# A hybrid decoder layer on one core: dense products placed between the steps of its RWKV-7 branch, and zeros, a scaling and stores moved

## The chip, the core and the metric

The kernel runs on one core of a Trainium2 chip. A core has five engines that each work through a queue of their own in order: PE (matrix products; the trace shows its weight loads apart, as PEld), DVE (elementwise work, reductions), ACT (activation functions and copies), POOL (elementwise work, zeroing) and SP (used here for issuing DMA transfers). [...] The metric is the device time of one execution in microseconds, lower is better.

## The reference, cut to what matters

One layer of a decoder for 512 prompt tokens and 64 tokens of eight running sequences (576 columns in all). The normalised input is multiplied with one large matrix `w_in`; of its columns, some feed an RWKV-7 branch, some a differential attention, some two sigmoid gates. Both branches are gated, added, multiplied with `w_out`, and a squared-ReLU MLP follows. The change lies in the RWKV branch and beside it:

```python
def step(S, inp):
    r_t, w_t, k_t, v_t, a_t, b_t = inp
    sa = jnp.einsum('bhij,bhj->bhi', S, a_t)
    S = S * w_t[:, :, None, :] + sa[..., None] * b_t[:, :, None, :] + v_t[..., None] * k_t[:, :, None, :]
    return S, jnp.einsum('bhij,bhj->bhi', S, r_t)
...
kk = kk / jnp.maximum(jnp.linalg.norm(kk, axis=-1, keepdims=True), 1e-12)
S, y = rwkv7_scan(S0, hs(r), hs(decay), hs(k), hs(v), -kk, kk * hs(a))
mean = jnp.mean(y, axis=-1, keepdims=True)
var = jnp.mean(jnp.square(y - mean), axis=-1, keepdims=True)
y = (y - mean) * lax.rsqrt(var + GN_EPS) * ln_x_w + ln_x_b
o = (y + bonus).reshape(B, T, W_A) * g
...
m = gate_a * (o_a @ lp['w_br_a']) + gate_b * (o_b @ lp['w_br_b'])
```

There are eight heads of 64, a state of 64 x 64 for each head and sequence.

## The kernel before, in words

Weights are streamed from memory in pieces of 512 columns. For each output block of 128 channels the generator `stream` (line 150 and on) loads the weights on SP's queue (`raw`), splits them on ACT and DVE into a rounded high part and a low part (`hi`, `lo`), and then *yields before each matmul*: 8 input blocks x 2 halves of 288 columns x 3 products (high x high, high x low, low x high) are 48 matmuls. These are the **dense products**; in the trace they write `ps_z` (columns of `w_in` for RWKV, function `shifted`), `ps_g` (gates, `gate`), `ps_brb` (output of the attention branch, `branch_b`), and later `ps_bra`, `ps_wo` and so on. Generators wait in a list, `waiting`, in one fixed order; each asks for the next only when the one before is spent, and the sums of one block go to one bank of accumulators, two banks in turn, so dense products never pass each other.

`take(n)` takes the next n dense products from the list where it stands in the program. Nothing binds them to that place: the planner that orders each engine's queue ahead of time walks the program in a simulation and gives an engine the next instruction that is ready there, so such products are drawn forward into any hole that the simulation sees. `fill(n)` does the same inside `tc.issue_after(ring["mm"].ins)`: its matmuls stand in PE's queue behind the last matmul that the program wrote before. `issue_after` orders a block's instructions that run on the same engine as the named one.

The eight heads are worked in four **pairs** (hp 0 to 3, the first to the fourth pair; two heads fill the 128 rows). `rwkv(hp)` is a generator with these stages, each ended by a `yield`:

- stage 0: squares of k, their sums per head on PE (`pn`), the power -1/2 on POOL (`nr`), spread to columns on POOL (`nb`), transposed on PE (`pk`); decay and gate terms (`pw`, `pa`, `u`, `aa`, a running sum `cum`); normalised keys `kk`, bonus sums (`rkp`, `pbn`, `bv`), and the products of keys within chunks of 64 tokens (`pA`, masked on DVE into `ABR` and `ST`). `ST` is zeroed in halves on POOL (line 818).
- stage 1: transposes of v (`pV`, into `SVU`) and of the keys (`pK`, into `KBt`), the starting states `s0` loaded and multiplied (`pI`), an identity block and zeros put into `SVU` on POOL (lines 871 and 872).
- stage 2: inversion of a triangular matrix by blocks of 32: `DT`, `Y`, `X`, then in four rounds `pW` and `pZ`, each followed by nine bound dense products (`blocks`); the result is `TT`, partly zeroed on POOL (lines 923 and 924).
- stage 3: states of the running sequences (`vm`, `pF`); stage 4: mean and variance of y (`var`, with a power on POOL, line 243); stage 5: scaling of y by var, transposes back (`pTy`), gating (`pg`), output.

`chain(pr)` walks the nine chunks of two pairs together, one after the other (`pch`, `pY`), each step needing the one before. At the end of the file's middle part a list written by hand sets the program order: `run(2, 3)` takes the next stage of hp 2 and of hp 3, and `take(n)` stands between. Before the change `fill(8)` stands after `pn` and after `pa` of stage 0 (for the third pair, `take(8)` instead), in stage 1 between `pV` and `pK` for the third and the fourth pair, and ahead of `pI` for the fourth (for the others `take(8)`).

`gate` stores each finished gate block to memory on SP's queue (line 452); they are read back much later.

Of the kernel before, what the change touches and what calls it, by code (L numbers as in the profile page):

```python
# [15 lines left out]
P = 128  # L16
# [20 lines left out]
C_ID, C_OB, C_M, C_MS, C_LM, C_I32, C_HS, C_SEL, C_MB, C_CM, C_END = (  # L37
    0, 128, 256, 384, 512, 672, 704, 706, 738, 746, 748)
# [3 lines left out]
def tile_hybrid_step(ctx, tc, xT, xsT, ktab, vtab, s0T, ptab, w_in, vecs, w2a2, g2, lamv,  # L42
                     w_bra, w_brb, w_out, w_up, w_down, cst, bias_p, bias_s,
                     yT, kTo, vTo, Sp, Ss, sh):
    nc = tc.nc
    PE, VE, AE, GE = nc.tensor, nc.vector, nc.scalar, nc.gpsimd
# [8 lines left out]
    ring = {"job": 0}  # L55

    def act(out, in_, func=AF.Copy, **kw):
        ring["act"] = AE.activation(out=out, in_=in_, func=func, **kw)  # L58

    def tt(out, a, b, op, eng=None):  # L60
        ins = (eng or VE).tensor_tensor(out=out, in0=a, in1=b, op=op)  # L61
        if eng is None:
            ring["tt"] = ins

    def stt(out, a, s, b, op0, op1):
        VE.scalar_tensor_tensor(out=out, in0=a, scalar=s, in1=b, op0=op0, op1=op1)

    def ts(out, a, s1, op0, s2=None, op1=ALU.bypass, eng=None):
        (eng or VE).tensor_scalar(out=out, in0=a, scalar1=s1, scalar2=s2, op0=op0, op1=op1)

    def mm(out, lhsT, rhs, start=True, stop=True):
        ring["mm"] = PE.matmul(out=out, lhsT=lhsT, rhs=rhs, start=start, stop=stop)  # L72
        return ring["mm"]
# [17 lines left out]
    MUL, ADD, SUB, MAX = ALU.mult, ALU.add, ALU.subtract, ALU.max  # L91
# [9 lines left out]
    def bank(name):  # L101
        return psw.tile([P, 512], F32, tag="w", name=name)

    def tbank(name):
        return psc.tile([P, 512], F32, tag="t", name=name)
# [6 lines left out]
    c = const.tile([P, C_END], F32, name="cst_sb")  # L112
# [21 lines left out]
    def v(i, n=1):  # L134
        return vec[:, i:i + n]
# [80 lines left out]
    def take(n):  # L216

        while waiting and n:
            if next(waiting[0], None) is None:
                waiting.pop(0)  # L220
            else:
                n -= 1

    def fill(n):

        with tc.issue_after(ring["mm"].ins):
            take(n)
# [37 lines left out]
    gt_d = tc.dram_tile([2 * KT, P, NT], F32, name="gt_d")  # L265
# [178 lines left out]
    def gate(g):  # L444

        gg = gs.tile([P, NT], F32, tag="gg", name=f"gg{g}")

        def ev(ps, t0, n):
            tt(gg[:, t0:t0 + n], ps, R1[:, t0:t0 + n], MUL)
            act(gg[:, t0:t0 + n], gg[:, t0:t0 + n], AF.Tanh, scale=0.5)  # L450
        yield from stream(w_in[26 + g], KT, xh, xl, HALF, ev, f"g{g}")
        nc.sync.dma_start(out=gt_d[g], in_=gg)

    def ob_halves():

# [209 lines left out]
    for h in range(HB):  # L665
        if h:
            qkv(h)
        for cc in range(2):
            GE.tensor_copy(
                out=qbd[64 * cc:64 * cc + 64, :, h, 8 * cc:8 * cc + 8],  # L670
                in_=qT[64 * cc:64 * cc + 64, h, NPR:].rearrange("p (b q) -> p b q", b=NB))
# [47 lines left out]
    def ch(a):  # L719
        return a.rearrange("p (c t) -> p c t", t=64)  # L720

    def m3(ap_, n):
        q, w = ap_.shape
        return ap_.rearrange("p (o w) -> p o w", o=1).broadcast_to([q, n, w])
# [17 lines left out]
    def rwkv(hp):  # L742
# [5 lines left out]
        def tmp(tag, bufs=1):  # L748
            return rt.tile([P, NT], F32, tag="T", name=f"{tag}_{hp}", bufs=6)


        sq = tmp("sq")
        act(sq, k, AF.Square, scale=v(V_KK + hp))
        pn = bank(f"pn{hp}")
        for t, o in enumerate(toks):
            mm(pn[:, 2 * t:2 * t + 2], sq[:, o:o + P], c[:, C_HS:C_HS + 2])
        (fill if hp != 2 else take)(8)
        nr = stat.tile([P, 10], F32, tag="nr", name=f"nr{hp}")
        ts(nr, pn[:, 0:10], 1e-24, MAX)
        GE.tensor_tensor(out=nr, in0=nr, in1=mhalf[:, :10], op=ALU.pow)  # L760

        nb = rt.tile([P, 5, P], F32, tag="G", name=f"nb{hp}", bufs=3)
        GE.tensor_copy(out=nb.rearrange("p t (a d) -> p (t a) d", a=2),
                       in_=nr.rearrange("p (a o) -> p a o", o=1).broadcast_to([P, 10, 64]))
        u = tmp("u")
        aa = tmp("aa")
        for t0, n in HALF:
# [3 lines left out]
            pa = bank(f"pa{hp}{t0}")  # L771
            mm(pa[:, :n], al[:, hs], Pt[12][:, t0:t0 + n])
            act(aa[:, t0:t0 + n], pa[:, :n], AF.Tanh, scale=0.5, bias=hw0[:, 4 + hp:5 + hp])
        (fill if hp != 2 else take)(8)
        ts(u, u, 1.0, ADD)
        cum = tmp("cum")
        VE.tensor_tensor_scan(out=cum, data0=reset, data1=u, initial=0.0, op0=MUL, op1=ADD)
# [36 lines left out]
        for par, rows in halves:  # L814
            stt(KB[rows, :, par], ch(aa)[rows], 0.5, ch(pinv)[rows], MUL, MUL)
            tt(KB[rows, :, 1 - par], ch(k2)[rows], ch(pinv)[rows], MUL)
            st = rb_.tile([P, NCH, 2, 64], F32, tag=f"ST{par}", name=f"ST{par}_{hp}")
            GE.memset(st[64 - 64 * par:128 - 64 * par], 0.0)
            stt(st[rows, :, 0], ch(kk)[rows], -1.0, ch(pm)[rows], MUL, MUL)
            tt(st[rows, :, 1], ch(r)[rows], ch(pe)[rows], MUL)  # L820
            ST.append(st)
# [4 lines left out]
        for par in range(2):  # L826
            rows = slice(64 * par, 64 * par + 64)
# [14 lines left out]
        SVU = own["SVU"][:, :, e]  # L842
        for cs, pV in two_chunks(f"pV{hp}", vv):
            for a, c0, c1 in cs:
                src = pV[64 * a:64 * a + 64].rearrange("p (c w) -> p c w", w=P)[:, :(c1 - c0 + 1) // 2]
                act(SVU[64:128, c0:c1:2, 0], src[:, :, 0:64])
                act(SVU[0:64, c0:c1:2, 1], src[:, :, 64:128])
        if hp >= 2:
            fill(8)
        KBt = rb_.tile([P, NCH, 2, 64], F32, tag="KBt", name=f"KBt{hp}")  # L850
        for c0, cn in ((0, 4), (4, 4), (8, 1)):
# [5 lines left out]

        s0 = rt.tile([P, NB, 64], F32, tag="s0", name=f"s0_{hp}")
        nc.sync.dma_start(out=s0, in_=s0T[hp])
        (fill if hp == 3 else take)(8)  # L860
        pI = bank(f"pI{hp}")
        for b in range(NB):
            for par, rows in halves:
# [2 lines left out]
        for par in range(2):  # L866
            rows = slice(64 * par, 64 * par + 64)
            for a in range(2):
                act(ST[par][rows, 8, a].rearrange("p (b t) -> p b t", b=NB),
                    pI[rows, 0:P].rearrange("p (b a t) -> p b a t", b=NB, a=2)[:, :, a])  # L870
            GE.tensor_copy(out=SVU[rows, 8, par], in_=c[rows, C_ID + 64 * par:C_ID + 64 * par + 64])
            GE.memset(SVU[rows, 0, par], 0.0)

        yield

# [10 lines left out]
        def blocks(ps, lhs, rhs, n):  # L886
            for ci in range(n):
                for g in range(4):
                    gs = slice(32 * g, 32 * g + 32)
                    last = mm(ps[gs, ci * 32:ci * 32 + 32], lhs[gs, ci], rhs[gs, ci])  # L890
            with tc.issue_after(last.ins):
                take(9)
            return ps[:, :n * 32].rearrange("p (c s) -> p c s", c=n)
# [3 lines left out]
        for l in range(1, 5):  # L897

            n = NCH if l < 3 else 8
            DM = rt.tile([P, NCH, 32], F32, tag="DM", name=f"DM{hp}_{l}")  # L900
            tt(DM[:, :n], DT[:, :n], m3(c[:, C_LM + 32 * l:C_LM + 32 * l + 32], n), MUL)
            W = rt.tile([P, NCH, 32], F32, tag="W", name=f"W{hp}_{l}")
            act(W[:, :n], blocks(tbank(f"pW{hp}{l}"), DM, X, n))
            tt(X[:, :n], X[:, :n], blocks(tbank(f"pZ{hp}{l}"), Y, W, n), ADD)
            VE.transpose(out=Y[:, :n], in_=X[:, :n])
        TT = rb_.tile([P, NCH, 64], F32, tag="TT", name=f"TT{hp}")
        pW = tbank(f"pWc{hp}")
# [11 lines left out]
        for b0, b1 in quads:  # L919
            act(TT[b0, :8, 32:64], pC[b0, :256].rearrange("p (c s) -> p c s", c=8))  # L920
            act(TT[b0, :, 0:32], Y[b0])
            act(TT[b1, :, 32:64], Y[b1])
            GE.memset(TT[b0, 8:, 32:64], 0.0)
            GE.memset(TT[b1, :, 0:32], 0.0)

        own[e] = ST, KBt, TT, ABR, pc
        yield
# [16 lines left out]
        y = own["y"][:, e]  # L944
# [4 lines left out]
        b9 = lambda a: a.rearrange("p (c o) -> p c o", o=1).broadcast_to([P, NCH, 64])  # L949
# [3 lines left out]
        var = stat.tile([P, NCH], F32, tag="var", name=f"var{hp}")  # L953
# [1 line left out]
        rpow(var, var, 1.0 / 64, 64e-5)  # L955

        yield
        tt(y, y, b9(var), MUL)
        oa = rt.tile([P, NT], F32, tag="G", bufs=3, name=f"oa{hp}")
        if hp >= 2:  # L960
            half_rows(hp)
# [79 lines left out]


    gens = [rwkv(hp) for hp in range(4)]

    def run(*stages):
        for hp in stages:
            while Pt[8 + hp] is None:
                take(2)
            next(gens[hp], None)

    waiting += zs(2) + zs(3) + [gate(g) for g in range(KT, 2 * KT)]
    ga = [gate(g) for g in range(KT)]
    waiting += ga[:5]
    run(0, 0)
    take(221)
    run(0, 1, 1)
    take(106)
    run(1)
    chain(0)
    run(2, 0, 1)  # L1060
    take(190)
    run(2, 3)
    take(85)
    run(2, 0, 1, 3)
    take(38)
    run(3)
# [21 lines left out]
    for d in range(KT):  # L1088
        g = []
        for i in range(2):  # L1090
            gg = rt.tile([P, NT], F32, tag="T", name=f"g{i}_{d}", bufs=6)
# [32 lines left out]
    for i, d in enumerate((0, 4, 1, 5, 2, 6, 3, 7)):  # L1124
# [31 lines left out]
        for j, (t0, n) in enumerate(HALF):  # L1156
            o = acc[:, t0:t0 + n]
# [142 lines left out]
    rows = []  # L1300
    for d, n in enumerate((None, "t1", "b11", "t2", "b21", "t3", "b22", "t4")):
        if n:
            t = fp.tile([P, 2, 4, 288], F32R, tag=f"h_{n}", name=f"w3_{d}", bufs=1)
            t = t.rearrange("p i k t -> p (i k t)")
# [179 lines left out]
```

## Time and profile before

| what | value |
|---|---|
| median of the timed runs | 1004.63 us (1004.32 to 1005.11, 3 runs) |
| the profiled execution's own time | 1006.88 us |
| its span, first to last instruction | 1005.1 us |
| PE busy | 975.1 us |
| DVE, ACT, POOL busy | 688.9, 497.0, 87.5 us |
| mean granted clock of PE | 0.993 |

A row of a group or of the timeline gives start and duration in microseconds, engine, line, operation, the tile written and the tiles read, their shapes, and how many instructions were merged (x4). In brackets stands the idle time of the engine just before, and what ended it. A row of a stretch gives, from one time to another, the busy time and the number of instructions of each engine, the granted clock of PE (1.00 is full), the share of the DMA engines and GB/s. Two matmul records of the trace belong to one product of 32-bit operands, one to a dense product. Matmuls overlap, so the start of one to the start of the next is what one costs.

### The profile page before, as it was taken

What the parts mean: (1) busy time and instruction counts of PE and PEld (TensorE: products, weight loads), DVE (VectorE), ACT (ScalarE), POOL (GpSimd) and SP (SyncE); (2) the same over time, 40 slices, a digit from 0 to 9 for tenths busy, and PEclk for the clock granted to TensorE, in tenths of its full rate; (3) what the DMA queues carried; (4) which work ended last, traced back from release to release, by engine and by line L of the source; (5) the groups of instructions that cost most, each with busy time, mean ns of one, the idle gap of its engine ahead of it and who ended that gap; (6) DMA issues with size and microseconds to landing.
All of it is one profiled execution on the core that took longest, in us unless ns stands there. A gap on an engine that the chain in (4) does not pass through costs nothing.

```text
span 1005.1 us, 24415 instructions
## 1 busy us (share of the span) xinstructions
PE 975.1 (97%) x10012; PEld 919.4 (91%) x10012; DVE 688.9 (69%) x1459; ACT 497.0 (49%) x1094; POOL 87.5 (9%) x171
## 2 busy tenths in 40 slices
PE   9999999899999998999989999999999999999996
PEld 9999998898887887988779999999999999999996
DVE  6698566864946679444579898966666666666644
ACT  6576455354435355453334666644444444444732
POOL 2511001301010340000210000000000000000001
PEclk9999999999989999999999999999999999999999
DMA  7422673211111234323357642222222222221402
GB/s 266 136 70 83 205 223 114 61 64 45 43 59 45 69 106 152 104 81 113 103 182 225 206 140 86 83 95 85 88 92 85 85 84 85 84 87 41 135 3 95
DMA packets 50833, 105.75 MB, mean 105 GB/s; under 512 B 6066, under 2 KB 8114, under 8 KB 50594
## 3 DMA queue, kind: packets, MB, share of 16 engines
q1 hardware_dynamic: 47442, 96.95, 30.4%
q0 software_dynamic: 1648, 5.35, 1.5%
q8 instruction: 79, 1.29, 0.5%
q10 hardware_dynamic: 1632, 1.89, 0.5%
q14 instruction: 32, 0.26, 0.1%
HBM read 89.38 MB, written 14.78 MB: 104 GB/s over the span
## 4 chain that ended last, share of the span: by engine, by line
PE 83%; DVE 6%; ACT 4%; issue 3%; DMA 2%; POOL 1%; SPq 0%; DVEq 0%; ACTq 0%; POOLq 0%
PE ps_dn L72 20%; PE ps_g L72 8%; PE ps_z L72 8%; PE ua L1220 5%; PE ux L1220 5%; PE ps_wo L72 4%; PE ps_k L72 3%; PE uc L1220 3%; PE ub L1220 3%; PE ud L1220 2%; PE ps_bra L72 2%; PE ps_q L72 2%; PE pch L72 2%; PE ps_brb L72 2%; PE ps_v L72 2%
## 5 line engine op out<-in xcount | busy, mean ns | idle before, releaser
L72 PE MATMUL ps_dn<-q,hi_dn 128*128 128x288 f32 x768 | 154.7, 296 | 0.0
L72 PEld LDWEIGHTS ps_dn<-q,hi_dn 128*128 128x128 f32 x768 | 122.7, 188 | 1.4
L72 PE MATMUL ps_dn<-q,lo_dn 128*128 128x288 f32 x384 | 113.2, 295 | 0.0
L72 PE MATMUL ps_g<-xl,hi_g 128*128 128x288 f32 x256 | 79.7, 311 | 0.0
L72 PE MATMUL ps_g<-xh,hi_g 128*128 128x288 f32 x256 | 79.0, 309 | 0.0
L72 PE MATMUL ps_g<-xh,lo_g 128*128 128x288 f32 x256 | 79.0, 309 | 0.0
L72 PEld LDWEIGHTS ps_dn<-q,lo_dn 128*128 128x128 f32 x384 | 72.0, 188 | 0.0
L72 PE MATMUL ps_z<-xh,lo_z 128*128 128x288 f32 (+1 forms) x224 | 68.9, 308 | 0.0
L72 PE MATMUL ps_z<-xh,hi_z 128*128 128x288 f32 (+1 forms) x224 | 67.6, 302 | 0.0
L72 PE MATMUL ps_z<-xl,hi_z 128*128 128x288 f32 (+1 forms) x224 | 66.8, 298 | 0.0
L61 DVE TENSOR_TENSOR ya<-ya,ps_dn 128x288 f32<-128x288 f32 x96 | 43.2, 451 | 29.4 <-PE ps_dn L72 29.4
L58 ACT ACTIVATE hi_dn<-raw_dn 128x512 fp32r<-128x512 f32 x48 | 30.1, 628 | 57.0 <-PE ps_dn L72 57.0
L1220 PE MATMUL ua<-h_b,hi 128*128 128x288 f32 x256 | 53.2, 298 | 0.0
L1220 PE MATMUL ux<-h_t,hi 128*128 128x288 f32 x256 | 52.3, 296 | 0.0
L58 ACT ACTIVATE c<-c 128x288 f32<-128x288 f32 x112 | 48.4, 439 | 7.4 <-DVE c L61 5.8
L72 PEld LDWEIGHTS ps_g<-xh,hi_g 128*128 128x128 f32 x256 | 48.7, 190 | 3.1 <-issue 1.8
L72 PEld LDWEIGHTS ps_g<-xl,hi_g 128*128 128x128 f32 x256 | 48.6, 190 | 1.9
L72 PEld LDWEIGHTS ps_g<-xh,lo_g 128*128 128x128 f32 x256 | 48.6, 190 | 1.6 <-DVE lo_g L61 0.2
L58 ACT ACTIVATE hi<-a 128x1024 fp32r<-128x1024 f32 (+1 forms) x32 | 27.1, 846 | 42.0 <-PE ps_dn L72 34.2
L72 PE MATMUL ps_dn<-q,w 128*128 128x320 f32 (+1 forms) x336 | 46.3, 297 | 0.0
L61 DVE TENSOR_TENSOR lo<-s,hi 128x1024 fp32r<-128x1024 f32 x32 | 39.2, 1224 | 10.1 <-ACT hi L58 10.0
L72 PEld LDWEIGHTS ps_dn<-q,w 128*128 128x128 f32 x336 | 45.3, 190 | 0.1
(395 smaller groups left out, 2802.2 us busy)
## 6 DMA issues: line engine op xcount, KB each, us to landing
a<-in_w_up_dram SPq DMA_DIRECT2D x32, 512.0 KB, 3.4
raw_dn<-in_w_down_dram SPq DMA_DIRECT2D x64, 256.0 KB, 2.8
raw_g<-in_w_in_dram SPq DMA_DIRECT2D x32, 256.0 KB, 3.1
raw_z<-in_w_in_dram SPq DMA_DIRECT2D x28, 256.0 KB, 3.1
gt_d<-gg SPq DMA_DIRECT2D x16, 288.0 KB, 2.4
g<-gt_d SPq DMA_DIRECT2D x16, 288.0 KB, 3.6
kp<-in_ktab_dram SPq DMA_DIRECT2D x16, 256.0 KB, 4.5
vp<-in_vtab_dram SPq DMA_DIRECT2D x16, 256.0 KB, 3.8
```

Source lines behind the costliest of these rows:

```text
L58: ring["act"] = AE.activation(out=out, in_=in_, func=func, **kw)
L61: ins = (eng or VE).tensor_tensor(out=out, in0=a, in1=b, op=op)
L72: ring["mm"] = PE.matmul(out=out, lhsT=lhsT, rhs=rhs, start=start, stop=stop)
L1220: ring["mm"] = PE.matmul(out=ps[:, :288], lhsT=l[:, k], rhs=hb[blk][:, h, k], start=start and i == 0, stop=i == 11, skip_group_check=skip)
```

## The change

1. Second pair (hp 1): its stage 1 no longer stands right after its stage 0 but behind the floating products, of which there are 82 instead of 106; eight bound products are put between `pV` and `pK`, and the eight ahead of `pI` become bound.
2. Third pair: the two groups of eight in stage 0 become bound.
3. Fourth pair: eight bound products are put ahead of `pn`; the floating products after its stage 0 are 77 instead of 85.
4. The zeros of the first pair in `ST`, `SVU` and `TT`, and for all pairs the identity copy into `SVU`, are queued on POOL behind the copy `nb` that was written last. The other pairs' zeros are as before.
5. The scaling of y in stage 5 stands in an `issue_after` that names a matmul: for the first two pairs the last one of the third round of the inversion written last (`ring["mid"]`), for the other two the last matmul written.
6. `gate` stores on ACT's queue instead of SP's.

```diff
         yield from stream(w_in[26 + g], KT, xh, xl, HALF, ev, f"g{g}")
-        nc.sync.dma_start(out=gt_d[g], in_=gg)
+
+        nc.scalar.dma_start(out=gt_d[g], in_=gg)
...
+        def clear(a):
+
+            if hp:
+                GE.memset(a, 0.0)
+            else:
+                with tc.issue_after(ring["nb"].ins):
+                    GE.memset(a, 0.0)
...
         pn = bank(f"pn{hp}")
+        if hp == 3:
+            fill(8)
         for t, o in enumerate(toks):
             mm(pn[:, 2 * t:2 * t + 2], sq[:, o:o + P], c[:, C_HS:C_HS + 2])
-        (fill if hp != 2 else take)(8)
+        fill(8)
...
-        GE.tensor_copy(out=nb.rearrange("p t (a d) -> p (t a) d", a=2),
-                       in_=nr.rearrange("p (a o) -> p a o", o=1).broadcast_to([P, 10, 64]))
+        ring["nb"] = GE.tensor_copy(out=nb.rearrange("p t (a d) -> p (t a) d", a=2),
+                                    in_=nr.rearrange("p (a o) -> p a o", o=1).broadcast_to([P, 10, 64]))
...
-        (fill if hp != 2 else take)(8)
+        fill(8)
         ts(u, u, 1.0, ADD)
...
-            GE.memset(st[64 - 64 * par:128 - 64 * par], 0.0)
+            clear(st[64 - 64 * par:128 - 64 * par])
...
-        if hp >= 2:
+        if hp >= 1:
             fill(8)
         KBt = rb_.tile([P, NCH, 2, 64], F32, tag="KBt", name=f"KBt{hp}")
...
-        (fill if hp == 3 else take)(8)
+        (fill if hp in (1, 3) else take)(8)
         pI = bank(f"pI{hp}")
...
-            GE.tensor_copy(out=SVU[rows, 8, par], in_=c[rows, C_ID + 64 * par:C_ID + 64 * par + 64])
-            GE.memset(SVU[rows, 0, par], 0.0)
+            with tc.issue_after(ring["nb"].ins):
+                GE.tensor_copy(out=SVU[rows, 8, par], in_=c[rows, C_ID + 64 * par:C_ID + 64 * par + 64])
+            clear(SVU[rows, 0, par])
...
             tt(X[:, :n], X[:, :n], blocks(tbank(f"pZ{hp}{l}"), Y, W, n), ADD)
+            if l == 3:
+                ring["mid"] = ring["mm"]
             VE.transpose(out=Y[:, :n], in_=X[:, :n])
...
-            GE.memset(TT[b0, 8:, 32:64], 0.0)
-            GE.memset(TT[b1, :, 0:32], 0.0)
+            clear(TT[b0, 8:, 32:64])
+            clear(TT[b1, :, 0:32])
...
         yield
-        tt(y, y, b9(var), MUL)
+
+        with tc.issue_after((ring["mid"] if hp < 2 else ring["mm"]).ins):
+            tt(y, y, b9(var), MUL)
...
     take(221)
-    run(0, 1, 1)
-    take(106)
-    run(1)
+    run(0, 1)
+    take(82)
+    run(1, 1)
     chain(0)
     run(2, 0, 1)
     take(190)
     run(2, 3)
-    take(85)
+    take(77)
     run(2, 0, 1, 3)
```

## The prediction

> **What bounds the kernel now.** I read the page's shares and its chain first, then the stretches of the RWKV part one by one, and inside a stretch the timeline.
>
> ```profile
> span 1005.1 us, 24415 instructions
> PE 975.1 (97%) x10012; PEld 919.4 (91%) x10012; DVE 688.9 (69%) x1459; ACT 497.0 (49%) x1094; POOL 87.5 (9%) x171
> ...
> PE 83%; DVE 6%; ACT 4%; issue 3%; DMA 2%; POOL 1%; SPq 0%; DVEq 0%; ACTq 0%; POOLq 0%
> ```
>
> PE is the bound: 975.1 of 1005.1 us busy, 83% of the chain that ended last. No matmul is added or removed, so the change can only win or lose PE's idle time (30 us in all), time in which PE works at a lower clock, and nothing else. The stretches (columns: busy time and count of PE, PEld, DVE, ACT, POOL, then the granted clock) tell where PE loses time among the parts that the diff touches:
>
> ```profile
> 178.20:182.30 4.10, 1.46 (x10) 1.17 (x8) 2.51 (x3) 2.19 (x4) 4.07 (x5) 1.00 0.00 0
> 262.00:271.70 9.70, 9.64 (x77) 9.15 (x75) 9.47 (x20) 2.56 (x5) 0.10 (x1) 1.00 0.19 57
> 271.70:276.70 5.00, 3.77 (x62) 3.10 (x61) 4.12 (x12) 4.81 (x12) 0.00 (x0) 1.00 0.00 0
> 276.75:283.55 6.80, 6.80 (x120) 5.70 (x123) 2.48 (x7) 2.16 (x8) 2.67 (x2) 0.50 0.01 2
> 380.00:385.00 5.00, 3.18 (x21) 2.62 (x20) 4.94 (x9) 1.42 (x4) 0.00 (x0) 1.00 0.52 155
> 512.30:515.60 3.30, 3.30 (x14) 3.12 (x13) 3.06 (x6) 0.31 (x2) 0.18 (x1) 0.50 0.39 114
> 520.40:527.70 7.30, 5.79 (x36) 4.65 (x34) 5.33 (x11) 3.93 (x10) 0.00 (x0) 1.00 0.73 238
> ```
>
> Four places matter: 178.2 (PE idles 2.64 us, POOL works), 271.7 (PE idles 1.23 us of 5 among the second pair's transposes, then 6.8 us at clock 0.50), 380 (PE idles 1.82 us, DVE full), and the tail at 520.4 (PE idles 1.51 us).
>
> **The change part by part.**
>
> *Zeros of the first pair behind its norm (POOL).* The first place in the timeline:
>
> ```profile
> 176.16 0.80 POOL L711 DMA_DIRECT2D ob_d<-obs  x1 [1.33 <-DVE nr L69]
> 177.01 2.16 POOL L818 MEMSET ST<- 64x1152 f32 x2
> 179.14 2.18 POOL L760 TENSOR_TENSOR nr<-nr,mhalf 128x10 f32<-128x10 f32 x1
> 181.29 0.23 POOL L871 COPY SVU<-cst_sb 64x64 f32<-64x64 f32 x1
> 181.47 0.14 POOL L872 MEMSET SVU<- 64x64 f32 x1
> 181.56 0.71 POOL L763 COPY nb<-nr 128x640 f32<-128x640 f32 x1
> ...
> 182.32 0.66 PE L76 MATMUL pk<-cst_sb,nb 128*128 128x128 f32 x4 [2.66 <-POOL nb L763]
> ```
>
> DVE handed over nr before 176.16, yet the power began at 179.14, behind two zeroings of ST (2.16), and nb behind a copy and a zeroing of SVU (181.29 to 181.56, 0.27). Queued behind nb, they leave 2.16 + 0.27 = 2.4 us; the second pair's two SVU zeros, which are bound to nothing, may take 0.14 each in the gap: -2.2 us. PE then still waits 0.4 of its 2.66. Behind nb the zeros are wanted first by pA, which comes after pk and after most of this pair's work on DVE; POOL is 9% busy, so their new place costs nothing (2.2 if pA had to wait for them). DVE's kk is made from pk, so its chain moves too. Bounds: 0 (other zeros fill the gap) to -2.66 (the whole wait).
>
> *Second pair: transposes and states behind `take(82)` with two groups of eight.* Dense products before, by stretch (tiles ps_z, then ps_g):
>
> ```profile
> 249.70:262.00 12.30, 10.29 (x75) 10.04 (x75) 0.90 (x2) 1.00 0.13 44
> 262.00:271.70 9.70, 1.60 (x10) 1.39 (x10) 0.82 (x2) 1.00 0.19 57
> ...
> 262.00:271.70 9.70, 4.82 (x28) 3.90 (x28) 0.43 (x1) 1.00 0.19 57
> 271.70:279.50 7.80, 0.11 (x1) 0.00 (x0) 0.03 (x1) 0.82 0.00 0
> ```
>
> 75 + 10 + 28 = 113 of the 106 + 8 = 114 are spent before 271.7: they are not bound to a place, so PE takes them whenever it would wait, and none is left for the transposes. What follows:
>
> ```profile
> 273.40 1.20 PE L76 MATMUL pK<-cst_sb,KB 128*128 128x128 f32 x9 [0.43 <-ACT SVU L58]
> 275.41 1.11 PE L72 MATMUL pI<-ST,s 64*64 64x16 f32 x32 [0.81 <-ACT KBt L58]
> 276.25 0.47 DVE L884 STREAM_TRANSPOSE X<-Y 128x288 f32<-128x288 f32 x1
> 276.45 2.05 PE L72 MATMUL pn<-cst_sb,sq 128*128 128x2 f32 x10
> 278.36 1.31 PE L72 MATMUL pw<-P,wl 128*128 128x288 f32 x2
> 279.60 1.19 PE L72 MATMUL pW<-X,DM 32*32 32x32 f32 x72
> 281.12 0.44 PE L72 MATMUL ps_g<-xh,lo_g 128*128 128x288 f32 x1
> 281.36 0.44 PE L72 MATMUL ps_g<-xh,hi_g 128*128 128x288 f32 x1
> 283.17 0.97 PE L72 MATMUL pZ<-W,Y 32*32 32x32 f32 x72
> ...
> 285.46 0.82 PE L72 MATMUL pW<-X,DM 32*32 32x32 f32 x72
> 287.59 0.82 PE L72 MATMUL pZ<-W,Y 32*32 32x32 f32 x72
> ```
>
> X is ready at 276.25 + 0.47 = 276.72, but PE reaches its first product pW at 279.60: ahead of it stand the third pair's norms (pn) and its first pw, drawn forward into the hole, at half the clock (dense products start 0.24 apart at 281.12). Now eight dense products stand between pV and pK and eight before pI, and 82 float. At full clock one costs 10.29 us / 75 = 0.137. Terms:
>
> 1. pW starts when X is there: 276.72 against 279.60, -2.9.
> 2. Clock: pW to pZ took 3.57 us (279.60 to 283.17), the same step later 2.13 (285.46 to 287.59): -1.4, if sixteen dense products (2.2 us) in that stretch keep PE busy enough.
> 3. pn and pw of the third pair are paid later at full clock, by half of 2.05 and half of 1.31: +1.7, less the slack that the chain's gaps have; I take +1.6.
> 4. 106 - 82 = 24 fewer floating, 8 more bound: 16 products, 2.2 us, are pushed to the end of the list, where PE idles 7.30 - 5.79 = 1.5 us for the last pair's results; +0.7.
>
> Sum -2.0. X itself doesn't move: DVE is busy 9.47 of 9.70 us before it. Bounds: -3.7 (pn and pw hide in the gaps that the missing products leave at 262 to 271.7) to +3 (second rival).
>
> *Third pair: its two groups become bound (`take` to `fill`).* They wait for pn and pa of that pair, which PE has already issued by then (276.45, 278.36 above); 0. If pn comes late, the 190 floating products behind them wait with it, at most one pn and pw: +1.6, counted in 3.
>
> *Fourth pair: eight products ahead of its norm.* The third place:
>
> ```profile
> 367.11 1.99 POOL L760 TENSOR_TENSOR nr<-nr,mhalf 128x10 f32<-128x10 f32 x1 [8.62 <-PE ps_g L72]
> 369.15 0.72 POOL L763 COPY nb<-nr 128x640 f32<-128x640 f32 x1
> 370.33 3.55 POOL L243 TENSOR_TENSOR var<-var,mhalf 128x9 f32<-128x9 f32 x2 [0.46 <-DVE var L69]
> ...
> 372.15 0.76 DVE L61 TENSOR_TENSOR y<-y,var 128x576 f32<-128x576 f32 x1 [1.78 <-POOL var L243]
> 372.83 0.45 DVE L69 TENSOR_SCALAR u<-u 128x576 f32<-128x576 f32 x1
> ...
> 384.37 1.24 PE L72 MATMUL pbn<-rkp,cst_sb 128*128 128x288 f32 x4 [1.82 <-DVE rkp L66]
> ```
>
> PE waits for DVE here, DVE for POOL's var, and POOL takes var behind nr and nb. Eight products, 8 x 0.137 = 1.1 us, ahead of pn put nr, nb, var, y, u and the DVE work up to rkp later by as much, while `take(85)` to `take(77)` keeps PE's own count. PE waits longer at pbn: +1.1. Bounds: 0 (if POOL takes var first) to +1.1.
>
> *Scaling of y behind ring["mid"].* The queueing context binds only instructions of the engine of the instruction that it names. That one is a matmul on PE, the scaling is on DVE: no order is added, 0. Were it bound, DVE's 1.78 wait ahead of u would go.
>
> *Gate stores from SP to ACT.*
>
> ```profile
> 287.74 0.33 SPq L452 DMA_DIRECT2D gt_d<-gg  x1
> ...
> 0.74 0.41 ACTq L111 DMA_DIRECT2D vec<-in_vecs_dram  x1
> ```
>
> Sixteen issues cost ACT 0.41 each, 6.6 us, beside 497.0 busy. Behind the store wait ACT's next copies: W in the triangular steps and SVU in the chain, for which PE waits. The nine dense products after each step cover most of it. SP is freed from waiting for gg, but the list of PE's waits names no weight load of this part, so that gains nothing. I take +0.4; bounds 0 to 5 stores x 0.41 = +2.0 (those that fall into the steps).
>
> [...]
>
> **The sum:** -2.2 - 2.0 + 1.1 + 0.4 = -2.7 us. The profiled execution took 1006.88 us (span 1005.1 and 1.8 around it), so 1004.2 of its kind. It lies 2.25 us above the median of the timed runs, 1004.63; the difference put there gives 1001.9.
>
> **The rivals.**
>
> *A part of the gain isn't there (no change).* Either POOL fills its gap at 177 with the second pair's ST zeros, which were next in its queue after the first pair's and are bound to nothing: -2.7 + 2.2 = -0.5, 1004.1. Or the half-clock stretch at 276.75 is missing in the timed runs: -2.7 + 1.4 = -1.3, 1003.3. For the first speaks that such zeros did slip into gaps before (177.01, 181.29); against it that the second pair's came only after all of the first's. For the second speaks the 2.25 us between profile and median; against it, that the trace shows it.
>
> *Slower: the dense products run out at the second pair's pA, and the clock is halved there.* Only 82 - 75 = 7 are left for 262 to 271.7, where 38 were spent; 31 x 0.137 = 4.2 us of PE's 9.64 go. It decides if what is left (5.4 of 9.7, pA and transposes) is as little for the clock as 271.7 to 276.7 was. Then 6.8 us run at half rate, 3.4 us late, and terms 1 to 3 are gone: -2.2 + 3.4 + 0.7 + 1.1 + 0.4 = +3.4, 1008.0. Against it: at 178.2 PE was busy 1.46 of 4.10 us, and no lower clock followed.
>
> *Better.* The second half-clock stretch (512.3, 3.3 us) vanishes as well when the stretches move against it, half of 3.3 = -1.7, and the fourth pair's eight cost nothing (-1.1): 1001.9 - 2.8 = 999.1.
>
> *The scaling is bound after all:* -1.8 at u, 1000.1.
>
> **How the numbers follow.** Forecast 1001.9: 0.43. Part of the gain missing: 0.22. Slower: 0.13. Better: 0.18. Scaling bound: 0.04. Changes under 0.2% (2.0 us: about what a measurement of this kernel can tell from no change) are "same", so faster is below 1002.6. Faster: three quarters of the forecast's 0.43, and 0.18 + 0.04, gives 0.54; slower is the second rival, 0.13; the rest, 0.33, is the same. The range reaches from the better case, with some room for the bounds of term 3 (998.5), to 1006.5, short of the slower rival.
>
> **What would show it.** Right: POOL's nr of the first pair starts right after the ob_d issue and PE's wait at pk falls under 1 us; eight ps_g between pV and pK of the second pair, pW within 0.5 us of X, clock 1.00 there; the wait at pbn of the fourth pair grows to about 2.9. Wrong: ST zeros still ahead of the first nr; a half-clock stretch among the second pair's pA; var ahead of nr on POOL; y no longer ahead of u on DVE; ACT's stores between pW and W with PE idle behind them.

## The result, and the profile after

The changed kernel takes 1013.7 us (median of six runs, 1012.27 to 1015.26), the kernel before, run beside it, 1005.0 us (1004.32 to 1005.94). The ratio of the two is 1.008, with a 95% interval of 1.0069 to 1.0091: 8.7 us slower, where 2.7 us faster was forecast, and past the end of the range (1006.5). The profiled execution took 1015.26 us.

The page of the changed kernel, its span, the busy time of the engines and the shares of the chain that ended last:

```profile
span 1013.4 us, 24408 instructions
PE 979.2 (97%) x10012; PEld 922.6 (91%) x10012; DVE 690.3 (68%) x1459; ACT 498.0 (49%) x1094; POOL 90.4 (9%) x171
...
PE 79%; DVE 8%; ACT 4%; DMA 3%; issue 3%; POOL 2%; SPq 0%; DVEq 0%; POOLq 0%; ACTq 0%
```

The work is the same, 10012 matmul records, but PE is busy 4.1 us longer (979.2 against 975.1) and idle 4.2 us longer (34.2 of the span against 30.0). The stretches of the changed kernel at the first three places of the prediction (the last line is the third), and two that the prediction had not looked at, from 362.20 and 366.00 (columns as there):

```profile
178.27:182.00 3.73, 2.29 (x17) 2.00 (x16) 2.32 (x4) 2.18 (x4) 3.61 (x3) 1.00 0.00 0
262.00:271.42 9.42, 6.98 (x58) 5.94 (x58) 8.84 (x20) 4.00 (x10) 0.10 (x1) 1.00 0.08 29
271.42:276.00 4.58, 4.58 (x63) 4.39 (x62) 4.11 (x13) 3.82 (x11) 0.00 (x0) 1.00 0.22 61
...
362.20:366.40 4.20, 1.40 (x74) 1.15 (x73) 3.15 (x7) 1.17 (x3) 0.00 (x0) 0.94 0.61 184
366.00:376.10 10.10, 9.70 (x62) 9.26 (x63) 2.15 (x6) 2.74 (x8) 3.11 (x4) 0.50 0.10 26
376.10:393.00 16.90, 15.42 (x128) 14.44 (x127) 14.36 (x26) 8.45 (x16) 4.40 (x6) 1.00 0.33 98
```

The first three lines are what the change was aimed at, and there it works: PE idles 1.44 us at the first pair's norm instead of 2.64, and the second pair's transposes run without a gap and, in this execution, at full clock. The idle time of the second pair has moved ahead of them: from 262.00 on PE now idles 2.44 us between the products of pA. The loss is elsewhere: at the third pair's pI PE idles 2.8 us of 4.2, and then works for 10.1 us at half its clock.

By the starts of the same instructions in the two traces, the changed kernel is ahead by 1.3 us at the second pair's pbn (259.29 against 260.59) and by 2.4 us at its pWc (296.70 against 299.15), behind by 2.3 us at the third pair's pA (346.23 against 343.91), by 6.7 us at the fourth pair's pk (378.24 against 371.52), by 8.4 us at its pWc (449.50 against 441.12), and by 10.4 us at the second chain's pF (509.01 against 498.64); the tail gives 2 us back, 1.6 of them between 511.96 and 520.37 us of the kernel before, which has a half-clock stretch there where the changed one has none.

**Where PE's time went.** For every matmul between 160 and 990 us I took the time to the start of the next one and subtracted the usual time of its kind in the kernel before. What is left falls into gaps over 0.3 us, losses inside half-clock stretches, losses of under 0.3 us where a dense product follows another kind of work or the other way round (a switch), and other small losses (us; the number of switches in brackets):

| kernel | gaps | half clock | switches | other small |
|---|---|---|---|---|
| before | 28.0 | 4.0 | 20.2 (303) | 64.2 |
| changed | 30.6 | 7.0 | 23.6 (331) | 63.7 |
| only_store | 30.5 | 7.4 | 22.7 (318) | 64.0 |
| all_but_store | 29.8 | 6.3 | 21.6 (304) | 63.3 |
| after_own_s | 25.6 | 4.5 | 23.4 (324) | 64.8 |
| clear_own_s | 23.2 | 4.9 | 20.3 (305) | 63.7 |
| pair2_own_s_vm | 27.2 | 1.6 | 22.2 (314) | 60.7 |

For the changed kernel the differences are +2.6, +3.0, +3.4 and -0.5, together about the 8.3 us by which its span is longer. What is called usual moves the split: with the median of each kind it is +3.4, +2.3, +3.0 and -0.3. So there are three losses of like size, known to about 1 us each.

*The finer weave.* What a switch costs, in PE's timeline of the kernel before (start, duration):

```profile
310.21 0.45 PE L72 MATMUL pY<-SVU,ABR 64*64 64x64 f32 x8
310.59 0.40 PE L72 MATMUL ps_g<-xh,hi_g 128*128 128x288 f32 x1
310.83 0.30 PE L72 MATMUL ps_g<-xl,hi_g 128*128 128x288 f32 x1
310.96 0.29 PE L72 MATMUL ps_g<-xh,lo_g 128*128 128x288 f32 x1
```

The first dense product behind pY takes 0.24 us until the next starts, the second 0.13: a switch costs 0.11. In the two chains the planner now puts the products into more and smaller groups: 331 switches against 303, of which 70 against 54 in the first chain and 76 against 62 in the second. The first chain also gets more of them. Its groups on the tile S on DVE before (durations in ns, then the starts of the first and the last in us):

```profile
L69 DVE TENSOR_SCALAR SVU<-S,pc x14: 221/241/244, 306.4 to 336.3; 64x64 f32<-64x64 f32 x14
L69 DVE TENSOR_SCALAR So<-S,pc x2: 246/246/246, 340.3 to 340.5; 128x64 f32<-128x64 f32 x2
```

and the gates' dense products in it, from pWc of the second pair to pA of the third (stretch, busy time and count of PE, PEld and DVE):

```profile
299.00:343.90 44.90, 26.27 (x145) 19.99 (x143) 2.90 (x7) 1.00 0.17 56
```

The same groups in the changed kernel:

```profile
L69 DVE TENSOR_SCALAR SVU<-S,pc x14: 237/241/248, 303.3 to 336.8; 64x64 f32<-64x64 f32 x14
L69 DVE TENSOR_SCALAR So<-S,pc x2: 248/248/248, 341.4 to 341.6; 128x64 f32<-128x64 f32 x2
```

and its stretch:

```profile
296.70:346.20 49.50, 32.05 (x172) 23.94 (x171) 3.19 (x7) 1.00 0.21 64
```

The chain starts 3.1 us earlier (303.3 against 306.4) and ends 1.1 us later: 38.1 us in place of 33.9, with 171 weight loads of dense products in place of 143.

*The wait for s0.* These 28 products are missing afterwards: 9 of them between the third pair's pA and the first pair's pF, and 19 in the stretch behind. From pF of the first pair to pI of the third, the dense products before (columns as just now):

```profile
351.38:364.44 13.06, 8.79 (x59) 7.87 (x58) 1.35 (x3) 1.00 0.44 144
```

and in the changed kernel:

```profile
353.51:366.40 12.89, 6.51 (x40) 5.34 (x39) 0.68 (x2) 0.98 0.39 128
```

The stretch has the same length, 13.06 and 12.89 us, because a series of steps sets it that the dense products run beside: pF, the new state on DVE, its store, and only then the load of the third pair's s0 into the same buffer. The load is issued at 359.44 before and at 361.49 after, and lands 4.9 and 4.8 us later. 58 products cover it before, but for 0.66 us; 39 do not. What SP's queue waited for ahead of its loads of s0 in the changed kernel, from 325 to 372 us (us in total, times, longest):

```profile
SPq L870 <- DMA out_Ss_dram<-s: 4.0, 2, 3.5
```

and PE's timeline there:

```profile
362.81 0.79 PE L72 MATMUL pW<-X,DM 32*32 32x32 f32 x68
366.40 1.89 PE L72 MATMUL pI<-ST,s 64*64 64x16 f32 x32 [2.81 <-DMA s<-in_s0T_dram]
```

*Stops inside pZ.* The wait for s0 is not the only gap that grew. PE's waits from 160 to 990 us before (us in total, times, longest):

```profile
PE pZ L72 <- issue: 1.5, 4, 0.9
...
PE pI L72 <- DMA s<-in_s0T_dram: 0.7, 1, 0.7
```

and in the changed kernel:

```profile
PE pZ L72 <- issue: 3.5, 4, 1.8
PE pI L72 <- DMA s<-in_s0T_dram: 2.8, 1, 2.8
```

Both grow by 2 us; longer waits for DVE (2.2 us) and shorter ones for ACT and POOL (2.7 us) about cancel. The two longest of the stops marked "issue" stand in the middle of a group of pZ, with its inputs ready, and end at 414.31 and 439.67. A packet of 16 KB of the DMA queue that the profile marks "instruction" landed at 412.83 and at 438.30. In the 17 traces together there are 52 such stops of over 0.3 us, and every one ends 1.2 to 1.5 us after the landing of such a packet. It looks as if PE had run out of its own instructions there, among many short matmuls; no run tests it.

*The clock.* Behind that wait for s0 the clock is at 0.50 from 366.0 to 376.1 (the line of the stretches above); there is a second such stretch at 393. The two last 10.24 and 3.41 us; the kernel before has one of 6.8 us at 276.7 and one of 3.4 us at 512.3. What sets their places and lengths no run shows.

### The profile page after: what moved, and what is told of

Read it like the earlier page. It is cut to its first block, busy times and chain, and to the rows that moved or that the text cites. A ratio compares the mean times of both kernels' runs of the same rounds, so it can differ in the third digit from the quotient of the medians.

```text
span 1013.4 us, 24408 instructions
## 1 busy us (share of the span) xinstructions
PE 979.2 (97%) x10012; PEld 922.6 (91%) x10012; DVE 690.3 (68%) x1459; ACT 498.0 (49%) x1094; POOL 90.4 (9%) x171
## 4 chain that ended last, share of the span: by engine, by line
PE 79%; DVE 8%; ACT 4%; DMA 3%; issue 3%; POOL 2%; SPq 0%; DVEq 0%; POOLq 0%; ACTq 0%
PE ps_dn L72 20%; PE ps_g L72 8%; PE ps_z L72 8%; PE ua L1236 5%; PE ux L1236 5%; PE ps_wo L72 4%; PE ps_k L72 3%; PE uc L1236 3%; PE ub L1236 3%; PE ud L1236 2%; PE pch L72 2%; PE ps_q L72 2%; PE ps_v L72 2%; PE ps_brb L72 1%; PE pY L72 1%
## 5 line engine op out<-in xcount | busy, mean ns | idle before, releaser
L72 PE MATMUL ps_g<-xh,hi_g 128*128 128x288 f32 x256 | 81.5, 318 | 0.0
L61 DVE TENSOR_TENSOR lo<-s,hi 128x1024 fp32r<-128x1024 f32 x32 | 39.2, 1225 | 10.2 <-ACT hi L58 10.0
```

## The experiments

The theory after the comparison, O: the moved instructions, above all the gate stores, make the planner lay out the dense products anew behind them, and three things there carry the loss: the weave, the wait for s0, the clock behind it. Its rivals: I, the stores cost ACT time and hold up its next copies; R, the second pair's new order is the loss; and P, added when the first four traces were read, DVE is held up by POOL.

**The parts alone.**

```diff
 only_store: the kernel before, and
-        nc.sync.dma_start(out=gt_d[g], in_=gg)
+        nc.scalar.dma_start(out=gt_d[g], in_=gg)
 all_but_store: the changed kernel, and the reverse of this
```

> The kernel before with one part of the change: the sixteen gate stores leave from ACT instead of SP. Theory O (order): the move lets the planner place the dense products otherwise, fewer of them stand between pF and pI of the third pair, PE idles there for the load of s0, and the clock is halved behind the idle stretch: slower by 2 to 7 us, the wait ahead of pI over 1.5 us (0.82 before), granted clock below 1.00 between 360 and 380 us. Theory I (issue): the stores cost ACT their issue time and hold up what ACT does next: slower by 2 to 7 us with pI's wait still near 0.8 us and the clock at 1.00 there. Theory R (reorder): the loss comes from the second pair's new order and not from the stores: within 1 us of the time before.

> The whole change except that the gate stores stay on SP. Theories O and I: the loss goes with the stores, the time is 1 to 3 us below the kernel before (the 1.3 us at the first pair's norms and what the second pair gives). Theory R: it stays 6 to 9 us above the kernel before.

only_store: 1015.06 us, ratio 1.0105 (1.0073 to 1.0137). This one line alone costs about 10 us, more than the whole change and than either theory had said. PE's order is that of the kernel before up to 301.16 us (13 us behind the first store) and another from there on. all_but_store: 1010.15 us, ratio 1.0053 (1.0038 to 1.0069): the rest costs 5 us as well. The parts don't add up, and neither O nor R holds alone. PE's longest waits of only_store from 345 to 395 us:

```profile
PE pA L72 <- DVE ST L61: 2.6, 1, 2.6
PE pI L72 <- DMA s<-in_s0T_dram: 2.3, 1, 2.3
PE pbn L72 <- DVE rkp L66: 1.3, 1, 1.3
```

The wait ahead of pI is there, over the 1.5 us that O asked for, and a half-clock stretch of 3.4 us behind it; none of the waits is for ACT, and from 160 to 990 us PE waits 3.8 us for ACT in all, against 5.3 in the kernel before. In the changed kernel a store takes ACT 0.33 to 0.35 us, and six of the sixteen are issued while the instruction before still runs: counted only where ACT does nothing else, they take 3.4 us of its queue in all. That is less than the 6.6 us from which the prediction started, and it isn't where the 10 us are. Ahead of pI there is a longer wait, though, for DVE's ST.

```diff
 only_clear: the kernel before, with clear() and ring["nb"] (item 4 of the change)
 only_pair2: the kernel before, with item 1
 only_pair4: the kernel before, with item 3
```

> The kernel before with the first pair's zeros placed behind nb on POOL and nothing else. All theories: nr starts 1.2 to 1.4 us earlier and the time falls by 1.3 us (0.8 to 1.6). If the 1.3 us are swallowed later, it is within 0.3 us of the time before.

> The kernel before with the second pair's part alone (82, 8 and 8 dense products in place of 106 and 8). Theories O and I: within 1.5 us of the time before, the prediction's own term for it being -2.0. Theory R: slower by 6 to 9 us, with the half-clock stretch behind pI of the third pair.

> The kernel before with the fourth pair's part alone (eight dense products ahead of pn, 77 in place of 85). By the prediction's step: var goes ahead or nr comes 1.1 us later, slower by 1.1 us (0 to 2). If the plan behind it changes as it did for the second pair: slower by 3 us or more.

only_clear: 1003.91 us, ratio 0.9985 (0.9971 to 0.9998), a gain of some 1 to 1.5 us as expected. only_pair2: 1008.57 us, 1.0031 (1.0015 to 1.0047), between the two theories: a part that was to give 2 us costs 3 to 4, without a half-clock stretch behind pI. only_pair4: 1004.67 us, 0.9995 (0.9974 to 1.0016): no difference.

```diff
 after_less_two: the changed kernel, and
-        fill(8)
+        (fill if hp != 2 else take)(8)          (twice, in stage 0)
-        with tc.issue_after((ring["mid"] if hp < 2 else ring["mm"]).ins):
-            tt(y, y, b9(var), MUL)
+        tt(y, y, b9(var), MUL)
```

> The changed kernel without the third pair's two fills and without the edge at the scaling of y. The prediction has both at nothing: the same order of instructions on every engine and the time of the changed kernel, 1013.7 us, within 2 us. If either acts: another order and another time.

1013.47 us, 1.0075 (1.0048 to 1.0101), and the instructions stand in the same order on every engine: items 2 and 5 of the change do nothing, as predicted.

**DVE held up by POOL.** The timeline of all_but_store, DVE and then POOL:

```profile
337.99 0.74 DVE L61 TENSOR_TENSOR ST<-P,pe 64x576 f32<-64x576 f32 x1
338.76 4.39 DVE L66 SCALAR_TENSOR_TENSOR ST<-sq,u 64x576 f32<-64x576 f32 x1
...
337.35 2.16 POOL L754 MEMSET ST<- 64x1152 f32 x2
339.49 3.04 POOL L61 TENSOR_TENSOR vm<-SVU,cst_sb 128x512 f32<-128x512 f32 x3
342.59 2.16 POOL L754 MEMSET ST<- 64x1152 f32 x2
```

and its stretches (PE, PEld, DVE, ACT, POOL, clock):

```profile
341.70:346.20 4.50, 1.45 (x12) 1.22 (x10) 4.34 (x6) 0.63 (x1) 3.78 (x7) 1.00 0.20 58
346.80:350.20 3.40, 3.40 (x17) 3.40 (x17) 3.27 (x8) 1.33 (x3) 0.00 (x0) 0.54 0.47 143
```

An instruction that took 0.75 us for the other head takes 4.39, and it ends only after POOL's three vm have. During POOL's zeroing, which reads nothing, DVE's ST took its 0.74. PE waits (1.45 us busy of 4.50) and then has a half-clock stretch. In the kernel before vm starts only during the last of ST's instructions; these take 0.74 to 0.76 us each, and the three vm take 3.55 us in place of 3.04. In only_store one of ST's instructions takes 4.1 us, in only_pair2 two take 1.5 each, in the changed kernel 1.5 and 1.6, for which PE waits 0.6 us there: it is a loss of the parts more than of the whole. Where DVE waits longest, in all_but_store and only_store (4.39 and 4.12 us), its record ends behind the last of three vm; in only_pair2 and in the changed kernel POOL is held up as well, and the three vm take 4.57 and 4.14 us in place of 3.04. What decides who waits the traces don't show: DVE's record begins 0.73 us ahead of POOL's first vm in all_but_store and 0.79 us ahead in only_pair2, where it takes 1.49.

```diff
 all_but_store_vm: all_but_store, and
-               ...broadcast_to([P, NB, 64]), MUL, GE)
+               ...broadcast_to([P, NB, 64]), MUL)
```

> The whole change with the gate stores left on SP, and the products vm computed by DVE in place of POOL. Theory P (DVE's work on ST is stretched, 4.39 us in place of 0.74, while POOL runs vm): the stretched instruction is back at 0.74 to 0.80 us, PE's 3.26 us of idle among the third pair's pA and the half-clock stretch behind it go, and the time falls by 2 to 5 us from 1010.15, unless vm, now behind DVE's other work, makes pF late. Rival (DVE waited for PE or ACT there): it still takes over 3 us.

1007.71 us, 1.0022 (1.0008 to 1.0036), some 2.4 to 3 us better. PE's order up to the end of pA is that of all_but_store; DVE's row in the timeline:

```profile
339.46 0.76 DVE L66 SCALAR_TENSOR_TENSOR ST<-sq,u 64x576 f32<-64x576 f32 x1
```

and the stretch:

```profile
341.00:347.00 6.00, 6.00 (x52) 6.00 (x52) 5.74 (x10) 1.87 (x4) 2.22 (x6) 1.00 0.36 122
```

4.39 us have become 0.76, PE idles nowhere in these 6 us, and the clock is full. P holds.

**The wait for s0.**

```diff
 after_own_s: the changed kernel, and
-        sn = s0
+        sn = rt.tile([P, NB, 64], F32, tag="G", bufs=3, name=f"sn{hp}")
 clear_own_s: only_clear, and the same
```

> The changed kernel, with the new state of the first pair written to a buffer of its own, so that the third pair's load of s0 need not wait for the store of the first pair's state. Theory O: PE's wait ahead of the third pair's pI falls from 2.99 us to under 0.5, no half-clock stretch begins there (10.24 us of it in the changed kernel, worth 3 to 5 us), and the time falls by 4 to 7 us, to 1007 to 1010 us. Rival (the chains' finer weave and the queues carry the loss): the wait goes and the time falls by less than 2 us.

> The kernel before with the first pair's zeros behind nb and the new state in a buffer of its own. PE's order up to the third pair's pF is that of the kernel before; the wait ahead of its pI (0.82 us before) goes: 1.5 to 2.5 us faster than the kernel before.

after_own_s: 1008.69 us, 1.0037 (1.0022 to 1.0052), 5 us better than the changed kernel, inside the 4 to 7 expected. PE's order up to pF is that of the changed kernel. The dense products between pF and pI:

```profile
355.36:364.71 9.35, 6.42 (x40) 5.34 (x39) 0.68 (x2) 1.00 0.45 133
```

and, of all work, the stretch that was at half clock:

```profile
366.00:376.10 10.10, 9.46 (x67) 8.70 (x66) 4.80 (x12) 5.21 (x13) 7.41 (x8) 1.00 0.04 15
```

The same 39 products fill 9.35 us instead of 12.89, and the clock stays full. In the table gaps fall by 5.0 us (2.8 of them are this wait, 2.2 the stops marked "issue") and the loss at half clock by 2.5, while the switches stay (324), 3.2 us over the kernel before. The time remains 3.3 us over it. That the switches are this remainder is argued from the table, not shown: no run takes them away, and the gaps are by now 2.4 us below those of the kernel before. clear_own_s: 1001.38 us, 0.996 (0.9945 to 0.9976), faster than both kernels, 4.0 us below the kernel before where 1.5 to 2.5 were expected. In the table its gaps are 4.8 us less. The wait at the first pair's pk falls from 2.66 to 1.44 us and that for s0 (0.66) is gone, as meant; the wait for pbn falls from 1.82 to 1.19, one of 1.18 ahead of a pTy at 509.61 is gone, and one of 1.17 ahead of the second chain's pF is new. What the buffer does in this company stays open: only_clear, in which PE's order is that of the kernel before throughout, has no wait for s0 in its trace either: from pF to pI it takes 12.41 us with 58 dense products, clear_own_s 12.40 with 58. The spans of the two traces differ by 0.8 us, the medians by 2.5.

**The stores again, and the rest on top.**

```diff
 store_clear_own_s: clear_own_s with the gate stores on ACT
 clear_own_s_vm: clear_own_s with vm on DVE
 pair24_own_s_vm: clear_own_s_vm with items 1 and 3
 pair2_own_s_vm: clear_own_s_vm with item 1
```

> The kernel clear_own_s (zeros behind nb, new state in its own buffer) with the gate stores moved to ACT. If the stores' loss is the wait for s0 and the clock behind it alone: within 1 us of clear_own_s, 1001.4 us. If the finer weave of the first chain and DVE's stretched ST count as well: 2 to 6 us above it, 1003.5 to 1007.5 us, with the first chain's eight steps 36.8 us long (33.9 in the kernel before) and no wait over 0.5 us ahead of the third pair's pI.

> The kernel clear_own_s with vm on DVE. There ST's instructions take their 0.74 to 0.76 us already, so nothing is to be had from them: within 1 us of clear_own_s. If pF, behind DVE's other work, comes late: 1 to 3 us slower.

> The whole change except the stores, with the new state in its own buffer and vm on DVE: the stretched ST and the wait for s0 are both taken away. If these two carried the loss of the second pair's part, its predicted gain shows: 999 to 1001 us, below clear_own_s. If something else ate it (PE's wait for the fourth pair's pbn, 2 us in all_but_store): 1002 to 1005 us.

> The kernel clear_own_s with vm on DVE and the second pair's part. If the fourth pair's part was what ate the gain in pair24_own_s_vm: 999 to 1001 us. If it is DVE's order, in which the fourth pair's KB stands ahead of rkp here too: 1002 to 1004 us, with PE waiting 1.5 us or more for pbn's rkp.

store_clear_own_s: 1007.75 us, 1.0031 (1.0018 to 1.0045). Without any wait for s0 the stores' new place still costs 6 to 7 us. The first chain takes 36.8 us, as expected, ST is stretched once more (345.72, 3.05 us in place of 0.75, beside two vm) and PE waits 1.60 us for it, 1.95 us elsewhere for DVE, and 0.73 for pbn, where clear_own_s waits 1.19 us at pbn and for none of the others.

clear_own_s_vm: 1001.6 us, 0.9971 (0.9956 to 0.9985), as clear_own_s: vm's place matters only where it meets ST. pair24_own_s_vm: 1003.56 us, 0.9995 (0.9977 to 1.0013); against the kernel before nothing is lost any more, but it lies 2 us above clear_own_s_vm, where a gain was expected. PE waits for the fourth pair's pbn here:

```profile
384.68 1.24 PE L72 MATMUL pbn<-rkp,cst_sb 128*128 128x288 f32 x4 [1.74 <-DVE rkp L66]
```

pair2_own_s_vm: 1000.39 us, 0.9962 (0.9948 to 0.9975): without the fourth pair's part, the second pair's costs nothing, and may gain 1 us over clear_own_s_vm (the intervals overlap). The fourth pair's eight products, harmless in the kernel before, cost 3 us in this company.

```diff
 pair2_own_s_vm_rkp: pair2_own_s_vm, with DVE's products KB behind rkp (for all pairs, aa for the fourth)
 pair4_own_s_rkp: clear_own_s with item 3 and the same
+            with tc.issue_after(rk_.ins):
+                tt(KB[rows, :, 1 - par], ch(k2)[rows], ch(pinv)[rows], MUL)
```

> As pair2_own_s_vm, with DVE's KB products held behind rkp. If DVE's order ate the gain: from the third pair's pk to the fourth pair's pbn 13 us or less (16.3 us in pair24_own_s_vm, 11.7 us in clear_own_s), and 1 to 3 us below pair2_own_s_vm. If not: as pair2_own_s_vm, within 1 us.

> The kernel clear_own_s with the fourth pair's part and KB held behind rkp. only_pair4 was within 0.2% of the kernel before, with rkp behind four KB products: with them out of the way 0 to 2 us below clear_own_s (999.4 to 1001.4 us). Rival: pA, late then by the KB products, gives it back: 1001 to 1003 us.

What was expected of these two fell, on both sides: 1009.71 us, 1.0059 (1.0038 to 1.0079), and 1006.34 us, 1.0012 (1.0 to 1.0025). From the fourth pair's pk to its pbn pair2_own_s_vm_rkp takes 13.2 us, pair2_own_s_vm 13.4, and new waits stand elsewhere; the longest of pair2_own_s_vm_rkp from 345 to 392 us:

```profile
PE pF L72 <- DVE vm L61: 2.5, 3, 1.5
PE ps_g L72 <- DVE lo_g L61: 2.5, 1, 2.5
PE pbn L72 <- DVE rkp L810: 1.0, 1, 1.0
```

Holding a few instructions of DVE back changed the order of everything behind them once more, and by more than was at stake. That KB ahead of rkp is what eats the gain in pair24_own_s_vm is therefore not shown.

## Why the prediction was wrong, point by point

- **Gate stores from SP to ACT (+0.4, at most +2.0): the step that failed.** It priced ACT's issues (6.6 us; they take 3.4 us of its queue, and PE waits 3.8 us for ACT from 160 to 990 us, 5.3 before) and took PE's order as given. But PE's order is planned from all of the program, and with the stores on another queue it is another from 301.16 us on: alone, that costs 10 us; on top of clear_own_s, 6 us.
- **Second pair (-2.0): failed as well, behind its own place.** There it did what was said: eight products between pV and pK, full clock, and the third pair's pn behind pI. The full clock (term 2) was luck, though: after_less_two, with the same order, has a half-clock stretch of 3.41 us there (columns as in the stretches above):

```profile
276.85:280.25 3.40, 3.40 (x79) 2.23 (x78) 1.11 (x2) 1.71 (x4) 2.21 (x2) 0.50 0.02 5
```

  and after_own_s one of 6.83 us from 277.43. How much work of PE is enough for the full clock, on which the term hung, no run shows. pW still starts 1.8 us behind X (275.57 + 0.48 against 277.87), not within 0.5. At pWc the changed kernel is 2.4 us ahead, 1.1 of it from here. Behind it the order of the first chain and of vm against ST is another, and alone the part costs 3 to 4 us. With vm and s0 out of the way (pair2_own_s_vm) it costs nothing.
- **Zeros of the first pair (-2.2): right in its mechanism, the size off.** The timeline of the changed kernel, POOL, DVE and PE's pk:

```profile
176.23 0.80 POOL L712 DMA_DIRECT2D ob_d<-obs  x1 [1.34 <-DVE nr L69]
177.02 0.37 POOL L755 MEMSET SVU<- 64x64 f32 x2
177.48 1.99 POOL L771 TENSOR_TENSOR nr<-nr,mhalf 128x10 f32<-128x10 f32 x1
179.53 1.57 POOL L774 COPY nb<-nr 128x640 f32<-128x640 f32 x1
...
179.23 1.36 DVE L788 TENSOR_TENSOR_SCAN cum<-reset,u 128x576 f32<-128x576 f32 x1
...
181.15 0.66 PE L76 MATMUL pk<-cst_sb,nb 128*128 128x128 f32 x4 [1.44 <-POOL nb L774]
```

  nr starts 1.7 us earlier, behind two zeros of SVU as the prediction allowed. But nb takes 1.57 us in place of 0.71, because it now falls under DVE's running sum, which reads two tiles: 0.86 us of the gain go there, and 1.2 are left; PE still waits 1.44 us, not under 1. In the 13 traces in which nb falls under this sum it takes 1.57 to 1.59 us, in the other four 0.71. It looks like the same meeting of DVE and POOL.
- **Third pair (0) and scaling of y (0): right**, the order without them is the same. That the scaling might be bound after all fell with it.
- **Fourth pair (+1.1).** POOL does take nr, nb and var in that order, and later (timeline of the changed kernel):

```profile
372.79 1.99 POOL L771 TENSOR_TENSOR nr<-nr,mhalf 128x10 f32<-128x10 f32 x1 [11.89 <-DVE nr L69]
374.84 0.72 POOL L774 COPY nb<-nr 128x640 f32<-128x640 f32 x1
...
376.11 3.55 POOL L243 TENSOR_TENSOR var<-var,mhalf 128x9 f32<-128x9 f32 x2
...
392.96 2.09 PE L72 MATMUL pbn<-rkp,cst_sb 128*128 128x288 f32 x4 [1.48 <-DVE rkp L66]
```

  Yet PE waits 1.5 us at pbn, not 2.9, and alone the part costs nothing: in only_pair4 nr comes only 0.12 us later (367.23 against 367.11), DVE's lo_g and var stand in another order, and PE waits 1.4 us at pbn in place of 1.8.
- **The slower rival** named a real sign, PE idle among the second pair's pA (2.44 us of 9.42, 8 products there in place of 38), but the clock stayed at 1.00 there, and its price, 1008.0, doesn't explain 1013.7. Of the better rival the half-clock stretch at 512.3 did vanish, which made the loss 1.6 us smaller; why it did no run shows. Neither these nor any other rival had the order of work further on as its mechanism. The chances were drawn as if the sum's terms were the only unknowns; a gain of 2.7 us stood against a replanned order whose stake is 5 to 10 us, so the 0.13 for slower was far too low.

What is shown: the stores alone cost 10 us, and in the changed kernel the buffer that takes the wait for s0 away gives back 5 of the 8.7 us (after_own_s), with half clock and stops inside pZ behind it among them. What is argued: that the finer weave is the rest, and that PE's stops inside pZ (3.1 us between 400 and 450 us) are waits for its own instructions. Open is why the planner's order is worse with the stores on ACT; that another order would avoid the losses with the stores there was not tried.

## What to carry to other kernels

Where a planner lays out the queues, a moved instruction isn't priced by its own duration: first find which covers are nearly used up (here 58 dense products over a series of steps that needs 13 us) and which work costs time when it meets (here POOL's vm and DVE's work on ST, 0.75 us stretched to 4.39), since a new order spends them blindly. Take such a cover out of the race before tuning the order: in the changed kernel a buffer of its own for the new state gave 5 us. And test parts one by one but also together, for here they don't add: +10.2, +3.7, -0.9 and -0.7 made +8.7.

## What the runs showed of the hardware

- DVE's instructions on ST, which read two tiles, took longer beside POOL's vm, which reads two as well: in place of 0.75 us 3.05 in store_clear_own_s, 4.12 in only_store and 4.39 in all_but_store, and in the last two to behind the third vm; 1.49 each in only_pair2, 1.49 and 1.60 in the changed kernel. With vm on DVE (all_but_store_vm) it was 0.76. A POOL copy under a DVE running sum went from 0.71 to 1.57 us. Beside POOL's zeroing, ST's instructions took 0.74 to 0.76 us.
- Where PE was busy 1.4 of 4.2 us (changed kernel, 362.20), 10.24 us at half clock followed; where it waited 1.1 us ahead of pI (only_pair2), none did. The same wait was followed by half clock in one trace and not in another: behind the wait of 2.7 us ahead of the first pair's pk there are 3.41 us of it in only_store and only_pair2 and none in the kernel before (PE busy 1.46 of 4.10 us there, clock 1.00 up to 276.7) and in only_pair4.
- Each of PE's 52 stops that the profile puts down to "issue" (over 0.3 us, 17 traces) ended 1.2 to 1.5 us after a 16 KB packet of instructions had landed.
- Changing between dense products and the chains' small ones costs 0.11 us where it was looked at, and all such changes together 20 to 24 us between 160 and 990 us.
